# Two transformer blocks in one kernel: three token-major products in 512-column blocks, and sliding attention's value parts side by side

## The chip, the cores and the metric

The kernel runs on one core of a Trainium2 chip. The metric is device time in microseconds (us), the median of several executions. The engines are TensorE (PE, matrix products and transposes; its weight loads are shown as PEld), VectorE (DVE), ScalarE (ACT), GpSimd (POOL) and SyncE (SP, which issues most DMAs). PE writes its results to PSUM, which has eight banks of 512 float32 columns.

## The reference, cut to what matters

Two blocks run one after the other on 512 tokens of width 1024, batch 1, all in float32. The change touches the first block's mixer and its attention to a memory of 256 rows:

```python
def hybrid_mixer(x, w_in, ...):
    proj = x @ w_in
    ml_qk, ml_v, ml_o, ml_i, ml_f, sw_q, sw_k, sw_v = jnp.split(proj, IN_SPLITS, axis=-1)
    ml_qk = jax.nn.silu(causal_dwconv(ml_qk, ml_conv_w, ml_conv_b))
    ml_q, ml_k = jnp.split(ml_qk, 2, axis=-1)
    h_ml = mlstm(ml_q, ml_k, ml_v, ml_o, ...)        # 4 heads of 128; sigmoid(ml_o) gates the result
    h_sw = sliding_window_attention(sw_q, sw_k, sw_v, swa_sinks, rel_bias)   # 8 heads of 64, 2 value heads
    return jnp.concatenate([h_ml, h_sw], axis=-1) @ w_out

def memory_cross_attention(x, mem, wq, wkv, wo):
    q = (x @ wq).reshape(B, S, XA_HEADS, XA_HEAD_DIM)
    k, v = jnp.split(mem @ wkv, 2, axis=-1)
    ...
```

In the sliding attention a block of 128 tokens sees itself and the block before it, so block 0 has one block of keys and blocks 1 to 3 have two. The values and gate (`ml_v`, `ml_o`) are 512 columns each, memory's values are 1024.

## The kernel before

A large product is made of split operands. `split` (L111) makes a high part by an ACT copy that rounds, and a low part by a DVE subtraction; `mm3` (L137) then sums three passes in PSUM: high x high, high x low, low x high. Weights come from HBM in pieces of 1 MB into one of three `raw` buffers, issued by SP (`load_cols`, L101). `split_w` (L115) splits them into tiles `wh` and `wl` of 1024 columns, for each of which there are five buffers (`WB`, L91).

Values, gate and memory's values are token-major: the activations are the stationary operand, the weights the moving one. `tm_block` (L611) takes 256 columns: one load, two splits of four row blocks each, and `tm_cols` (L189), which computes two token tiles of 128 side by side in one bank, over all eight row blocks for one and then for the other. The values take two such blocks (`v_evac`, L595, an ACT copy into `vml`), the gate two (`o_evac`, L602, a tanh on ACT and a DVE operation into `og`), memory's values four (a split into `xvh`, `xvl`).

The sliding attention has eight groups, four token blocks by two value heads (`sw_group`, L520). A group makes scores of four heads in two banks with tag "s" (tile `sws`), a biased and negated copy with its minimum on DVE (L536, tile `swl`, three buffers), exponentials with sums on ACT (L541), a sum and a reciprocal on DVE (L543, L544), a scaling on POOL (L546), transposes on PE into a bank with tag "pt" (L551, tile `swpt`), their split (`swpth`, `swptl`), and the product with the values by `mm3` into the bank with tag "o" (tile `swop`). Of `swop`, DVE copies the upper and ACT the lower 64 partitions to `swo` (L562). The values `swv` were split at the start by `kv_evac` (L416), each head's 64 columns written twice, for the two halves of the partitions.

While the first mixer runs, the banks are: "mm" 0, 1, 2; "s" 3, 4; "pt" 5, 6; "o" 7 (`psm`, L342). `Banks` hands the banks of a tag out in turn, in the order in which the program names the tiles. The program's order is: projections of the sliding attention, its eight groups, values, gate, the query and key projections of the mixer's heads 0 and 1 (`cm_phase`, tile `cm`), memory's transposes, then for each head `ml_head` (L649; scores `mls`, numerators `num` in two "pt" banks, transposed result `htr` in the next "pt" bank) with memory's keys (`mem_key`, tile `mk`) between, then memory's values, then the mixer's output projection (`tm_rotate`, tile `tm`, all eight banks).

The order on each engine is not the program's: the compiler's scheduler plans it ahead with a timeline of its own, and takes of the instructions that are ready the one that stands first in the program. On the chip each engine then runs its list in order.

Of the kernel before, what the change touches and what calls it, by code (L numbers as in the profile page):

```python
# [8 lines left out]
F32 = mybir.dt.float32  # L9
F32R = mybir.dt.float32r  # L10
AF = mybir.ActivationFunctionType
OP = mybir.AluOpType
# [3 lines left out]
P = 128  # L16
T = 512
NT = T // P
D = 1024
KC = D // P  # L20
# [21 lines left out]
def tile_two_blocks(ctx: ExitStack, tc: tile.TileContext, a: dict, out: bass.AP, dbg=None):  # L42
    nc = tc.nc
    pe, act, dve, pool, sp = nc.tensor, nc.scalar, nc.vector, nc.gpsimd, nc.sync
# [48 lines left out]
    def raw_tile(name):  # L93
        return rawp.tile([P, 2112], F32, name=name, tag="raw", bufs=RAWB)
# [16 lines left out]
    def split(hi, lo, src):  # L111
        act.activation(hi, src, AF.Copy)  # L112
        dve.tensor_sub(lo, src, hi.bitcast(F32))  # L113

    def split_w(src, pl=None):  # L115
        shape = list(src.shape)
        n = 1
        for s in shape[1:]:
            n *= s
        if pl is None:  # L120
            hi = w_tile("wh")[:, :n]
            lo = w_tile("wl")[:, :n]
        else:
            pl, i = pl
            hi = pl.tile([P, n], F32R, name=f"wxh{i}")
            lo = pl.tile([P, n], F32R, name=f"wxl{i}")
        if len(shape) == 3:
            hi = hi.rearrange("p (k c) -> p k c", k=shape[1])
            lo = lo.rearrange("p (k c) -> p k c", k=shape[1])
        split(hi, lo, src)  # L130
        return hi, lo
# [5 lines left out]
    def mm3(ps, wh, wl, xh, xl, first, last):  # L137
        pe.matmul(ps, wh, xh, start=first, stop=False)  # L138
        pe.matmul(ps, wh, xl, start=False, stop=False)  # L139
        pe.matmul(ps, wl, xh, start=False, stop=last)  # L140
# [198 lines left out]
    w_in = a["w_in"][0]  # L339
    A0 = act_set(apool0, "x")  # L340
    psm = Banks(mm=(0, 1, 2), s=(3, 4), pt=(5, 6), o=(7,))
# [4 lines left out]
    mlq = open_pool("mlq", side="right")  # L346
    sw = open_pool("sw", side="left")
# [27 lines left out]
    swo = ml.tile([P, 4, T], F32, name="swo")  # L375
# [17 lines left out]
    while d0 < P:  # L393
        b = t5_bucket(d0)
# [10 lines left out]
    normg = sw.tile([P, T], F32, name="normg")  # L405
# [2 lines left out]


    swkt = [[sw.tile([P, P + T], F32R, name=f"swk{j}{i}") for i in range(2)] for j in range(2)]  # L410
    swv = [[sw.tile([P, 2, P], F32R, name=f"swv{t}{i}") for i in range(2)] for t in range(NT)]
    swk = [sw.tile([P, 2, 2, P], F32, name="swk", tag="swptl", bufs=2) for _ in range(2)]
    swk = [swk[t // 2][:, t % 2] for t in range(NT)]
    gates = [sw.tile([P, 8], F32, name=f"gates{t}") for t in range(NT)]

    def kv_evac(t, ps):  # L416
        kin = ps[:, 0:128].rearrange("p (j o d) -> p j o d", j=2, o=1).to_broadcast([P, 2, 2, 64])
        vin = ps[:, 128:256].rearrange("p (j o d) -> p j o d", j=2, o=1).to_broadcast([P, 2, 2, 64])
        dve.tensor_copy(gates[t], ps[:, 256:264])
        dve.tensor_copy(swk[t].rearrange("p j (u d) -> p j u d", u=2), kin)  # L420
        split(*[v.rearrange("p j (u d) -> p j u d", u=2) for v in swv[t]], vin)

    pst = Banks(tr=(3, 4, 5, 6), v=(7,))
    to_cm(pst, "tr", 4, xr[0][:, 0, :], A0, 0)
# [1 line left out]
    for k0, k1 in ((0, 3), (3, 6), (6, 8)):  # L426
        wh, wl = [w_tile(n)[:, :(k1 - k0) * 264].rearrange("p (k c) -> p k c", k=k1 - k0) for n in ("wh", "wl")]
        for j in range(0, k1 - k0, 2):
            e = min(j + 2, k1 - k0)
# [19 lines left out]
    for j in range(2):  # L449
        ps = psm.tile([P, T], F32, name="ktr", tag="pt", bufs=2)  # L450
# [6 lines left out]
    for g in range(2):  # L457
        ps = psm.tile([P, T], F32, name="gtr", tag="pt", bufs=2)
# [34 lines left out]
    ps = psm.tile([P, 14, 4], F32, name="actr", tag="pt", bufs=2)  # L493
# [26 lines left out]
    def sw_group(n, j):  # L520
        kbs = [0, 1] if n else [1]
        lo = 0 if n else P
        pts = {}
        Ps = []
        for cc in range(2):
            c = 2 * j + cc
            s = psm.tile([P, 2, 256], F32, name="sws", tag="s", bufs=2)
            for e in range(2):
                q = swq[2 * c + e][:, n * P:(n + 1) * P]
                for i in range(2):  # L530
                    pe.matmul(s[:, e, :], q, swkt[j][i][:, n * P:(n + 2) * P], start=i == 0, stop=i == 1)
            L = sw.tile([P, 2, 256], F32, name="swl", tag="swl", bufs=3)
            st = sw.tile([P, 5, 2], F32, name="swst", tag="swst", bufs=4)
            for e in range(2):
                h = 2 * c + e
                dve.tensor_tensor_reduce(L[:, e, lo:], s[:, e, lo:], swb[:, h, lo:], scale=-0.125,  # L536
                                         scalar=nsink[:, h:h + 1], op0=OP.add, op1=OP.min, accum_out=st[:, 1, e:e + 1])
            dve.tensor_sub(st[:, 2, :], st[:, 1, :], nsink[:, 2 * c:2 * c + 2])
            act.activation(st[:, 2, :], st[:, 2, :], AF.Exp)
            for e in range(2):  # L540
                act.activation(L[:, e, lo:], L[:, e, lo:], AF.Exp, scale=-1.0, bias=st[:, 1, e:e + 1],  # L541
                               accum_out=st[:, 3, e:e + 1])
            dve.tensor_add(st[:, 4, :], st[:, 3, :], st[:, 2, :])  # L543
            dve.reciprocal(st[:, 4, :], st[:, 4, :])  # L544
            for e in range(2):
                pool.tensor_scalar(L[:, e, lo:], L[:, e, lo:], st[:, 4, e:e + 1], 0.0, op0=OP.mult, op1=OP.add)  # L546
            Ps.append(L)
        for kb in kbs:
            pt = psm.tile([P, 4, P], F32, name="swpt", tag="pt", bufs=2)
            for h in range(4):  # L550
                pe.transpose(pt[:, h, :], Ps[h // 2][:, h % 2, kb * P:(kb + 1) * P], ident)  # L551
            pts[kb] = (sw.tile([P, 4, P], F32R, name="swpth", tag="swpth", bufs=2),
                       sw.tile([P, 4, P], F32R, name="swptl", tag="swptl", bufs=2))
            split(*pts[kb], pt)
        o = psm.tile([P, 2, 2, P], F32, name="swop", tag="o", bufs=1)
        for i, kb in enumerate(kbs):
            v, pt = swv[n - 1 + kb], [p.rearrange("p a b -> p (a b)") for p in pts[kb]]
            mm3(o.rearrange("p a b c -> p (a b c)"), v[0][:, j, :], v[1][:, j, :], pt[0], pt[1], i == 0,
                i == len(kbs) - 1)
        for e in range(2):  # L560
            r = slice(64 * e, 64 * e + 64)
            (act.copy if e else dve.tensor_copy)(swo[r, 2 * j:2 * j + 2, n * P:(n + 1) * P], o[r, :, e, :])  # L562

    NV = 31 + 3 + 3 + 4 + 4
    pv = consts.tile([P, 2, NV], F32, name="pv")
# [25 lines left out]
    og = ml.tile([P, 2080], F32, name="og", tag="og")[:, :NT * T].rearrange("p (t c) -> p t c", t=NT)  # L591
    vml = ml.tile([P, 2080], F32, name="vml", tag="vml").rearrange("p (t h c) -> p t h c", t=NT, h=4)
    pool.memset(vml[:, :, :, 128:130], 1.0)

    def v_evac(b):  # L595
        def f(t0, ps):
            for u in range(2):
                act.activation(vml[:, t0 + u, 2 * b:2 * b + 2, 0:128],
                               ps[:, u * 256:(u + 1) * 256].rearrange("p (h d) -> p h d", h=2), AF.Copy)
        return f  # L600

    def o_evac(b):  # L602
        def f(t0, ps):
            th = mlq.tile([P, 2, 256], F32, name="oth", tag="cy", bufs=2)
            act.activation(th, ps.rearrange("p (u c) -> p u c", u=2), AF.Tanh, scale=0.5)
            for u in range(2):
                dve.scalar_tensor_tensor(og[:, t0 + u, b * 256:(b + 1) * 256], th[:, u, :], 1.0,
                                         normg[:, b * 256:(b + 1) * 256], op0=OP.add, op1=OP.mult)
        return f

    def tm_block(w, c0, A, tt_n, psp, tag, bufs, evac):  # L611
        v = load_cols(w, c0, 256)
        ws = [split_w(v[:, k:k + 4, :]) for k in (0, 4)]
        tm_cols([(ws[k // 4][0][:, k % 4, :], ws[k // 4][1][:, k % 4, :]) for k in range(KC)], A, range(tt_n), 256,
                psp, tag, bufs, 2, evac)
# [18 lines left out]
            qk[c] = q  # L634
        return f

    for b in range(2):
        tm_block(w_in, 1024 + b * 256, A0, NT, psm, "mm", 3, v_evac(b))
    for b in range(2):
        tm_block(w_in, 1536 + b * 256, A0, NT, psm, "mm", 3, o_evac(b))  # L640
    dump("vml", vml)
    dump("og", og)

# [65 lines left out]
    M1 = act_set(apool1, "mem")  # L709
# [5 lines left out]
    wkv = a["xa_wkv"][0]  # L715
# [10 lines left out]
    for h in range(4):  # L726
        ps = ml_head(h)
# [19 lines left out]
    mlq.release()  # L747
    xvp = open_pool("xv")
    xvh, xvl = [xvp.tile([P, 2, D], F32R, name=f"xv{i}") for i in range(2)]
    for b in range(4):  # L750
        tm_block(wkv, D + b * 256, M1, 2, psm, "mm", 3,
                 lambda t0, ps, b=b: split(xvh[:, :, b * 256:(b + 1) * 256], xvl[:, :, b * 256:(b + 1) * 256],
                                           ps.rearrange("p (u c) -> p u c", u=2)))
    dump("h1h", H1[0].bitcast(F32))
    ml.release()

# [648 lines left out]
```

## Time and profile before

| | |
|---|---|
| time, median of 3 runs | 1320.43 us (1320.33 to 1323.15) |
| the profiled execution | 1322.3 us, of which its span 1320.6 |
| mean granted clock of PE | 0.994 |
| PE busy | 1300.4 us, 98% of the span, 6918 passes |
| DVE, ACT, POOL busy | 744.3, 534.2 and 76.1 us |

The views are read thus. A line of a timeline has the start in us from the span's start, the duration, the engine, the line of the kernel, the operation, the written and the read tiles by name, their shapes and a count. A PE pass is shown with a duration longer than its distance to the next one, since passes overlap. A line of a grouped view has busy time and mean duration of one (in ns) behind the first bar, and the engine's idle time before them behind the second.

### The profile page before, as it was taken

The page shows a single profiled execution, that of the slowest core. Times are in us where ns is not written, and L with a number is a line of the kernel's source. Part 1 is how long each engine was busy: PE and PEld are TensorE (multiplying, and loading weights), DVE is VectorE, ACT ScalarE, POOL GpSimd, SP SyncE. Part 2 cuts the span into 40 slices and gives each one's busy share as a digit, 9 for nine tenths or more (in the row PEclk, how much of TensorE's full clock was granted, in tenths as well). Part 3 has the DMA queues.
Part 4 walks back from the last instruction along what each step waited for, and adds up shares of the span by engine and source line. Part 5 has one row for each costly group of instructions (what it writes and reads, how often), then busy time and mean ns, then how long its engine had stood idle before and what let it go on. Part 6 is the DMA issues. An engine that isn't in the chain of part 4 may idle for free.

```text
span 1320.6 us, 17065 instructions
## 1 busy us (share of the span) xinstructions
PE 1300.4 (98%) x6918; PEld 1114.9 (84%) x6918; DVE 744.3 (56%) x1204; ACT 534.2 (40%) x895; POOL 76.1 (6%) x152
## 2 busy tenths in 40 slices
PE   8999999999999999999999999999999999999997
PEld 7899899899889888888888898767898888888886
DVE  5765877584666655556633569995453334532422
ACT  5664564333423433344422134576432223432311
POOL 3221020110000000000000120000100000000000
PEclk9999999998999999999999999999999999999999
DMA  8312344432223332313233124212234332223211
GB/s 255 108 65 73 104 144 160 181 109 97 97 96 116 124 128 64 128 64 128 70 122 128 32 69 138 73 45 93 73 93 125 96 96 97 96 96 112 96 46 51
DMA packets 92148, 134.87 MB, mean 102 GB/s; under 512 B 4572, under 2 KB 77329, under 8 KB 92062
## 3 DMA queue, kind: packets, MB, share of 16 engines
q1 hardware_dynamic: 90030, 129.09, 29.7%
q10 hardware_dynamic: 1384, 2.58, 0.6%
q0 software_dynamic: 656, 2.12, 0.5%
q8 instruction: 54, 0.88, 0.3%
q14 instruction: 24, 0.20, 0.0%
HBM read 131.66 MB, written 2.12 MB: 101 GB/s over the span
## 4 chain that ended last, share of the span: by engine, by line
PE 94%; DVE 3%; ACT 2%; issue 0%; DMA 0%; POOL 0%; SPq 0%; DVEq 0%; POOLq 0%; ACTq 0%
PE cm L139 15%; PE cm L138 15%; PE cm L140 15%; PE tm L224 9%; PE tm L223 9%; PE tm L227 9%; PE tmc L200 2%; PE tmc L201 2%; PE tmc L199 2%; PE tr L294 1%; PE tm L140 1%; PE tm L139 1%; PE tm L138 1%; PE num L680 1%; DVE cacc L1123 1%; PE mls L660 1%
## 5 line engine op out<-in xcount | busy, mean ns | idle before, releaser
L113 DVE TENSOR_TENSOR wl<-rawc,wh 128x1024 fp32r<-128x1024 f32 x140 | 170.7, 1222 | 203.6 <-ACT wh L112 203.3
L112 ACT ACTIVATE wh<-rawc 128x1024 fp32r<-128x1024 f32 x140 | 147.7, 1059 | 222.0 <-PE cm L139 190.8
L113 DVE TENSOR_TENSOR wl<-rawr,wh 128x1024 fp32r<-128x1024 f32 x73 | 88.9, 1223 | 147.4 <-ACT wh L112 147.4
L112 ACT ACTIVATE wh<-rawr 128x1024 fp32r<-128x1024 f32 x73 | 76.9, 1060 | 175.3 <-PE tm L227 126.6
L139 PE MATMUL cm<-x2l,wh 128*128 128x512 f32 (+1 forms) x392 | 143.8, 368 | 0.0
L140 PE MATMUL cm<-x2h,wl 128*128 128x512 f32 (+1 forms) x392 | 143.7, 367 | 0.0
L138 PE MATMUL cm<-x2h,wh 128*128 128x512 f32 (+1 forms) x392 | 143.1, 368 | 0.0
L139 PE MATMUL cm<-x4l,wh 128*128 128x512 f32 (+1 forms) x296 | 106.6, 361 | 1.3 <-DVE x4l L113 1.3
L140 PE MATMUL cm<-x4h,wl 128*128 128x512 f32 (+1 forms) x296 | 106.4, 360 | 0.0
L138 PE MATMUL cm<-x4h,wh 128*128 128x512 f32 (+1 forms) x296 | 105.9, 361 | 0.0
L140 PEld LDWEIGHTS cm<-x2h,wl 128*128 128x128 f32 x392 | 73.8, 189 | 12.1
L139 PEld LDWEIGHTS cm<-x2l,wh 128*128 128x128 f32 x392 | 73.8, 189 | 12.0
L138 PEld LDWEIGHTS cm<-x2h,wh 128*128 128x128 f32 x392 | 73.5, 189 | 12.3
L624 DVE SCALAR_TENSOR_TENSOR uy<-cm,fw,uy 128x511 f32<-128x511 f32 x88 | 65.5, 747 | 1.4
L138 PE MATMUL cm<-x3h,wh 128*128 128x512 f32 (+1 forms) x184 | 63.9, 352 | 1.1 <-DVE xc L624 0.8
L139 PEld LDWEIGHTS cm<-x4l,wh 128*128 128x128 f32 x296 | 55.8, 189 | 10.0 <-DVE x4l L113 1.5
L139 PE MATMUL cm<-x3l,wh 128*128 128x512 f32 (+1 forms) x184 | 64.1, 350 | 0.0
L140 PE MATMUL cm<-x3h,wl 128*128 128x512 f32 (+1 forms) x184 | 63.5, 347 | 0.0
L140 PEld LDWEIGHTS cm<-x4h,wl 128*128 128x128 f32 x296 | 55.8, 189 | 8.3
L138 PEld LDWEIGHTS cm<-x4h,wh 128*128 128x128 f32 x296 | 55.5, 189 | 8.5
L329 POOL TENSOR_TENSOR rs_r<-rs_e,mhalf 128x1 f32<-128x1 f32 (+1 forms) x16 | 24.2, 1510 | 540.5 <-DVE rs_e L328 540.5
L199 PE MATMUL tmc<-wh,xh 128*128 128x256 f32 (+1 forms) x160 | 47.2, 295 | 1.5 <-ACT wh L112 1.5
(457 smaller groups left out, 3058.2 us busy)
## 6 DMA issues: line engine op xcount, KB each, us to landing
rawc<-in_ffn_w_up_dram SPq DMA_DIRECT2D x22, 1024.0 KB
rawc<-in_w_in_dram SPq DMA_DIRECT2D x20, 1024.0 KB
rawc<-in_mlp_w_dram SPq DMA_DIRECT2D x16, 1024.0 KB
rawr<-in_mlp_w_dram SPq DMA_DIRECT2D x16, 1024.0 KB
rawr<-in_ffn_w_down_dram SPq DMA_DIRECT2D x11, 1024.0 KB
rawr<-in_w_out_dram SPq DMA_DIRECT2D x10, 1024.0 KB
rawc<-in_xa_wkv_dram SPq DMA_DIRECT2D x8, 1024.0 KB
rawc<-in_xa_wq_dram SPq DMA_DIRECT2D x4, 1024.0 KB
```

Of the source, the lines that this page charges most:

```text
L112: act.activation(hi, src, AF.Copy)
L113: dve.tensor_sub(lo, src, hi.bitcast(F32))
L138: pe.matmul(ps, wh, xh, start=first, stop=False)
L139: pe.matmul(ps, wh, xl, start=False, stop=False)
L140: pe.matmul(ps, wl, xh, start=False, stop=last)
L199: pe.matmul(o, xh, wh, start=k == 0, stop=False)
L200: pe.matmul(o, xh, wl, start=False, stop=False)
L201: pe.matmul(o, xl, wh, start=False, stop=k == KC - 1)
L223: pe.matmul(ps[t][h], xh, wh[:, c], start=i == 0, stop=False)
L224: pe.matmul(ps[t][h], xh, wl[:, c], start=False, stop=False)
L227: pe.matmul(ps[t][h], xl, wh[:, c], start=False, stop=i == n - 1)
L624: dve.scalar_tensor_tensor(dst[:, s:], ps[:, :T - s], w[:, j:j + 1], y[:, s:], op0=OP.mult, op1=OP.add)
```

## The change

Three things change.

- Values, gate and memory's values are computed by a new function, `tm_wide`, in blocks of 512 columns, one bank for each token tile. It loads half of the rows at a time (1 MB), splits two row blocks at once, and runs through all token tiles for each row block. The values use the banks "mm", "mm", "mm", "o", the gate "s", "s", "pt", "pt", memory's first column block "s", "s" and its second "pt", "pt".
- In the sliding attention the high and the low part of a value head stand side by side in 128 columns (one tile `swv` instead of two), so that one pass with the high and one with the low probabilities give the product of the high values in the upper and of the low values in the lower 64 partitions. Then ACT copies the lower half out, and two DVE additions add the halves into `swo`.
- The pool `sw` gets a small tile named "pad".

```diff
+    swv = [sw.tile([P, 2, P], F32R, name=f"swv{t}") for t in range(NT)]
...
+    sw.tile([P, 32], F32, name="pad")
...
+        vin = ps[:, 128:256].rearrange("p (j d) -> p j d", j=2)
...
+        v = swv[t].rearrange("p j (u d) -> p j u d", u=2)
+        split(v[:, :, 0, :], v[:, :, 1, :], vin)
...
         for i, kb in enumerate(kbs):
-            v, pt = swv[n - 1 + kb], [p.rearrange("p a b -> p (a b)") for p in pts[kb]]
-            mm3(o.rearrange("p a b c -> p (a b c)"), v[0][:, j, :], v[1][:, j, :], pt[0], pt[1], i == 0,
-                i == len(kbs) - 1)
+            for part in range(2):
+                pe.matmul(of, swv[n - 1 + kb][:, j, :], pts[kb][part].rearrange("p a b -> p (a b)"),
+                          start=i == 0 and part == 0, stop=i == len(kbs) - 1 and part == 1)
+        half_o = sw.tile([64, 2, 2, P], F32, name="swhalf", tag="swhalf", bufs=1)
+        act.copy(half_o, o[64:P])
         for e in range(2):
-            r = slice(64 * e, 64 * e + 64)
-            (act.copy if e else dve.tensor_copy)(swo[r, 2 * j:2 * j + 2, n * P:(n + 1) * P], o[r, :, e, :])
+            dve.tensor_add(swo[64 * e:64 * e + 64, 2 * j:2 * j + 2, n * P:(n + 1) * P], o[0:64, :, e, :],
+                           half_o[:, :, e, :])
...
+    def v_evac(t, ps):
+        act.activation(vml[:, t, :, 0:128], ps.rearrange("p (h d) -> p h d", h=4), AF.Copy)
+
+    def o_evac(t, ps):
+        th = mlq.tile([P, T], F32, name="oth", tag="cy", bufs=2)
+        act.activation(th, ps, AF.Tanh, scale=0.5)
+        dve.scalar_tensor_tensor(og[:, t, :], th, 1.0, normg, op0=OP.add, op1=OP.mult)
+
+    def tm_wide(w, c0, A, psp, banks, evac):
+
+        ps = [psp.tile([P, T], F32, name="tmw", tag=tag, bufs=bufs) for tag, bufs in banks]
+        for k0 in (0, 4):
+            v = raw_tile("rawv")[:, :4 * T].rearrange("p (k c) -> p k c", k=4)
+            sp.dma_start(v, w[k0 * P:(k0 + 4) * P, c0:c0 + T].rearrange("(k p) c -> p k c", p=P))
+            for k1 in (0, 2):
+                wh, wl = split_w(v[:, k1:k1 + 2, :])
+                for u in range(2):
+                    k = k0 + k1 + u
+                    for t, o in enumerate(ps):
+                        mm3(o, A[0][:, k, t * P:(t + 1) * P], A[1][:, k, t * P:(t + 1) * P], wh[:, u, :], wl[:, u, :],
+                            k == 0, k == KC - 1)
+        for t, o in enumerate(ps):
+            evac(t, o)
...
-    for b in range(2):
-        tm_block(w_in, 1024 + b * 256, A0, NT, psm, "mm", 3, v_evac(b))
-    for b in range(2):
-        tm_block(w_in, 1536 + b * 256, A0, NT, psm, "mm", 3, o_evac(b))
+    tm_wide(w_in, 1024, A0, psm, (("mm", 3), ("mm", 3), ("mm", 3), ("o", 1)), v_evac)
+    tm_wide(w_in, 1536, A0, psm, (("s", 2), ("s", 2), ("pt", 2), ("pt", 2)), o_evac)
...
-    for b in range(4):
-        tm_block(wkv, D + b * 256, M1, 2, psm, "mm", 3,
-                 lambda t0, ps, b=b: split(xvh[:, :, b * 256:(b + 1) * 256], xvl[:, :, b * 256:(b + 1) * 256],
-                                           ps.rearrange("p (u c) -> p u c", u=2)))
+    for b, tag in enumerate(("s", "pt")):
+        c = slice(b * T, (b + 1) * T)
+        tm_wide(wkv, D + b * T, M1, psm, ((tag, 2), (tag, 2)),
+                lambda t, ps, c=c: split(xvh[:, t, c], xvl[:, t, c], ps))
```

## Rows read from the trace of the kernel before

**Rows 1.** The page's chain of work that ended last: shares of the span by engine.

```profile
PE 94%; DVE 3%; ACT 2%; issue 0%; DMA 0%; POOL 0%; SPq 0%; DVEq 0%; POOLq 0%; ACTq 0%
```

**Rows 2.** Timeline of PE: start, duration, engine, line, out<-in, idle before.

```profile
118.77 0.28 PE L200 MATMUL tmc<-wl,xh 128*128 128x256 f32 x1
121.76 0.28 PE L201 MATMUL tmc<-wh,xl 128*128 128x256 f32 x1
...
170.05 0.40 PE L138 MATMUL cm<-xh,wh 128*128 128x512 f32 x1
173.93 0.39 PE L140 MATMUL cm<-xh,wl 128*128 128x512 f32 x1
```

**Rows 3.** PE by line, 50 to 122, then 205 to 233 us.

```profile
L199 PE MATMUL tmc<-wh,xh 128*128 128x256 f32 x128 | 37.1, 290 | 0.0
L531 PE MATMUL sws<-swk,swq 128*128 128x256 f32 x59 | 10.6, 289 | 1.3 <-DVE swq L515 1.3
L139 PE MATMUL swop<-swptl,swv 128*128 128x512 f32 x14 | 5.7, 404 | 0.0
...
L201 PE MATMUL tmc<-wh,meml 128*128 128x256 f32 x64 | 18.3, 285 | 0.0
```

**Rows 4.** Timeline, PE and ACT: first and last attention group's end, first projection.

```profile
66.49 0.39 PE L140 MATMUL swop<-swpth,swv 128*128 128x512 f32 x1
...
118.54 0.39 PE L140 MATMUL swop<-swpth,swv 128*128 128x512 f32 x1
...
119.42 0.37 ACT L562 COPY swo<-swop 64x256 f32<-64x256 f32 x1 [3.87 <-DVE swo L562]
...
121.88 0.40 PE L138 MATMUL cm<-xh,wh 128*128 128x512 f32 x1
```

**Rows 5.** Timeline of DVE, ACT and PE around the mixer's heads 0 and 1.

```profile
161.21 0.68 DVE L667 SCALAR_TENSOR_TENSOR pm<-mls,mle 128x512 f32<-128x512 f32 x1
165.18 0.60 DVE L694 SCALAR_TENSOR_TENSOR hn<-num,mv,og 128x128 f32<-128x128 f32 x2
...
177.85 0.58 ACT L737 ACTIVATE h0s<-htr 128x512 f32<-128x512 f32 x1
...
181.64 0.83 PE L680 MATMUL num<-vml,pm 128*128 128x130 f32 x6
```

**Rows 6.** All engines by line, 66.7 to 118.9 us: count, busy us, mean ns.

```profile
L546 POOL TENSOR_SCALAR swl<-swl,swst 128x256 f32<-128x256 f32 x22 | 11.0, 516 | 31.7 <-DVE swst L544 21.3 <-PE swpt L551 5.6 <-ACT swst L539 4.7
L541 ACT ACTIVATE swl<-swl,swst 128x256 f32<-128x256 f32 x20 | 10.0, 505 | 0.1
L113 DVE TENSOR_TENSOR swptl<-swpt,swpth 128x512 fp32r<-128x512 f32 x13 | 8.7, 685 | 3.0 <-ACT swpth L112 3.0
L536 DVE CUSTOM_DVE_ANT_0 swl<-sws,swb,nsink 128x256 f32<-128x256 f32 x20 | 8.7, 478 | 1.7 <-PE swpt L551 1.7
L112 ACT ACTIVATE swpth<-swpt 128x512 fp32r<-128x512 f32 x13 | 7.4, 595 | 4.2 <-PE swpt L551 4.1
L562 DVE COPY swo<-swop 64x256 f32<-64x256 f32 x7 | 2.9, 416 | 6.3 <-PE swop L140 6.3
L543 DVE TENSOR_TENSOR swst<-swst 128x2 f32<-128x2 f32 x10 | 1.4, 157 | 1.6 <-ACT swst L539 1.5
```

**Rows 7.** Timeline of PE, ACT, DVE: memory's first values, heads 2 and 3.

```profile
205.64 0.28 PE L199 MATMUL tmc<-wh,memh 128*128 128x256 f32 x1
208.27 1.05 PE L680 MATMUL num<-vml,pm 128*128 128x130 f32 x8
...
213.92 1.27 ACT L696 ACTIVATE hn<-hn,mf 128x128 f32<-128x128 f32 x4
...
229.09 0.60 DVE L694 SCALAR_TENSOR_TENSOR hn<-num,mv,og 128x128 f32<-128x128 f32 x2
```

**Rows 8.** Windows: length, busy (count) of PE, PEld, DVE, ACT, POOL; PE's clock; DMA.

```profile
850.00:860.00 10.00, 6.21 (x24) 3.03 (x22) 10.00 (x22) 5.77 (x11) 0.00 (x0) 1.00 0.54 204
860.00:870.00 10.00, 9.09 (x32) 6.84 (x33) 10.00 (x23) 5.04 (x10) 0.00 (x0) 0.83 0.01 2
```

More of the change, by code (lines that the diff above doesn't have):

```diff
@@ L410, in tile_two_blocks @@
     swkt = [[sw.tile([P, P + T], F32R, name=f"swk{j}{i}") for i in range(2)] for j in range(2)]
-    swv = [[sw.tile([P, 2, P], F32R, name=f"swv{t}{i}") for i in range(2)] for t in range(NT)]
+    swv = [sw.tile([P, 2, P], F32R, name=f"swv{t}") for t in range(NT)]
     swk = [sw.tile([P, 2, 2, P], F32, name="swk", tag="swptl", bufs=2) for _ in range(2)]
@@ L414, in tile_two_blocks @@
     gates = [sw.tile([P, 8], F32, name=f"gates{t}") for t in range(NT)]
+    sw.tile([P, 32], F32, name="pad")
     def kv_evac(t, ps):
         kin = ps[:, 0:128].rearrange("p (j o d) -> p j o d", j=2, o=1).to_broadcast([P, 2, 2, 64])
-        vin = ps[:, 128:256].rearrange("p (j o d) -> p j o d", j=2, o=1).to_broadcast([P, 2, 2, 64])
+        vin = ps[:, 128:256].rearrange("p (j d) -> p j d", j=2)
         dve.tensor_copy(gates[t], ps[:, 256:264])
         dve.tensor_copy(swk[t].rearrange("p j (u d) -> p j u d", u=2), kin)
-        split(*[v.rearrange("p j (u d) -> p j u d", u=2) for v in swv[t]], vin)
+        v = swv[t].rearrange("p j (u d) -> p j u d", u=2)
+        split(v[:, :, 0, :], v[:, :, 1, :], vin)
     pst = Banks(tr=(3, 4, 5, 6), v=(7,))
@@ L555, in sw_group @@
         o = psm.tile([P, 2, 2, P], F32, name="swop", tag="o", bufs=1)
+        of = o.rearrange("p a b c -> p (a b c)")
         for i, kb in enumerate(kbs):
-            v, pt = swv[n - 1 + kb], [p.rearrange("p a b -> p (a b)") for p in pts[kb]]
-            mm3(o.rearrange("p a b c -> p (a b c)"), v[0][:, j, :], v[1][:, j, :], pt[0], pt[1], i == 0,
-                i == len(kbs) - 1)
+            for part in range(2):
[3 more added lines that the diff above has]
+        act.copy(half_o, o[64:P])
         for e in range(2):
-            r = slice(64 * e, 64 * e + 64)
-            (act.copy if e else dve.tensor_copy)(swo[r, 2 * j:2 * j + 2, n * P:(n + 1) * P], o[r, :, e, :])
+            dve.tensor_add(swo[64 * e:64 * e + 64, 2 * j:2 * j + 2, n * P:(n + 1) * P], o[0:64, :, e, :],
+                           half_o[:, :, e, :])
     NV = 31 + 3 + 3 + 4 + 4
@@ L593, in tile_two_blocks @@
     pool.memset(vml[:, :, :, 128:130], 1.0)
[L595 to L609, printed above, removed]
+    def v_evac(t, ps):
[18 more added lines that the diff above has]
+            evac(t, o)
     def tm_block(w, c0, A, tt_n, psp, tag, bufs, evac):
```

## The prediction

> **What bounds the kernel now.** I read the page first, and in it the chain of work that ended last: TensorE (PE) carries 94% of it [rows 1]. So a microsecond of PE work taken out is a microsecond of time, as long as PE still finds other work in its place; and a microsecond for which PE runs dry is lost at once. Next I read the timeline of PE, for what one pass costs: from one start to the next, not by the duration shown, because the passes overlap. Last I read the two stretches that the change touches, 50 to 122 us and 205 to 233 us, by line, to see what lies between what.
>
> Start to start, 25 steps of a 256-column pass take 121.76 - 118.77 = 2.99 us, 0.1196 us each, and 17 steps of a 512-column pass take 173.93 - 170.05 = 3.88 us, 0.228 us each [rows 2]. A pass thus costs 0.108 us for 256 columns and about 0.012 us whatever its width.
>
> In the first stretch the 384 passes of values and gate (three lines of 128) stand between the score passes (59 of 64 lie in it), the 56 transposes and the value passes (three lines of 14) of the sliding attention [rows 3]. The first projection of queries follows the last of them at 121.88 [rows 4]. Until then PE never waits long: it takes a pass of values or gate whenever the attention, which stands earlier in the program, isn't ready. The attention's eight groups end their value passes from 66.9 (66.49 + 0.39) to 118.9 us (118.54 + 0.39) [rows 4]: seven steps of 7.4 us. PE's own work for a group of eight score passes, eight transposes and six value passes is only 8 x 0.12 + 0.96 (the transposes, put at what passes of 256 columns cost, more than they can) + 6 x 0.228 = 3.3 us. The attention is a long chain over four engines, and the 384 passes are its cover.
>
> **The change part by part.**
>
> Wide blocks: 384 passes become 192, 384 x 0.1196 - 192 x 0.228 = 2.1 us saved. Memory's values: 192 passes (three lines of 64 [rows 3]) become 96, 22.96 - 21.89 = 1.1 us saved. Value parts: 42 passes become 28, 14 x 0.228 = 3.2 us saved. Together 6.4 us of PE work.
>
> Here a rule of the Trainium skill speaks against the first two. It gives a warm pass as its columns over the clock plus about 2.5 ns (page "TensorE: Matmul & The Clock Gate", section "Wait — 56ns, not 53.3ns?"); by that, merging 288 pairs would save 0.7 us, an estimate from that page, where the rows give 2.1 + 1.1. The rows decide; the fixed part in this kernel is five times the page's.
>
> The order of the banks is where I part from the plain sum. The fourth value tile lies in bank 7 (tag "o"), which every attention group uses, and all eight groups stand ahead of it in the program. The gate's four tiles lie in the banks of the scores and of the transposed probabilities. Does a later tile get a bank that lies empty while an earlier one isn't ready? The mixer's heads answer. Head 1's second numerator uses the bank of head 0's first one. Head 0's last reading of its numerators ends at 165.78, and head 1's first operand was written at 161.89, yet its first six passes come at 181.64, after head 0's transposed result, which uses that bank in between, was copied out at 178.43 [rows 5]. The bank waited 16 us for its turn. I take it that banks go in program order.
>
> Then this follows. Three value tiles (banks 0 to 2) fill PE with 72 passes, 72 x 0.228 = 16.4 us. The fourth, 24 passes, waits for the last attention group to be copied out, and until its passes run none of the four split value weights is free. There are five buffers for these; the fifth takes the gate's first quarter, and the other three quarters, and all query projections behind them, wait. Gate passes on that first quarter (24) can run once score and transpose banks are free, in the attention's last group. So under the attention lie 16.4 + 5.5 us of cover in place of 46 us, and behind its end at F stand 24 value passes and 72 gate passes: 96 x 0.228 = 21.9 us. The query projections start at F + 21.9; now they start at 121.88. The break-even for this stretch is F = 100.0; now bank 7 is copied out at 119.79 [rows 4].
>
> How far does the attention shorten when PE is free for it? A chain sets a lower end: two score reductions on DVE, 0.96 us; two exponentials on ACT, 1.01; a sum and a reciprocal, 0.31; the scaling on POOL, 1.03 [rows 6]; eight transposes, 0.96: 4.3 us from one group's transposes to the next's, since with three buffers for the scores the next group's second half starts only then. DVE sets another: four reductions at 0.478, six small ones of about 0.157, two splits at 0.685, a copy at 0.416 [rows 6], 4.6 us. The change replaces DVE's copy and ACT's copy (0.37 [rows 4]) by an ACT copy of 64x512, bounded by 0.37 and the 0.6 of a 128x512 activation, and two DVE additions, each put like the copy, 0.416 [rows 6]; so DVE has 5.1 us a group. The upper end is 7.4, the step as it is. I take 5.1, DVE's sum: three PE steps of a chain no longer queue behind fillers, and most of the eight weight splits that lay between have moved behind it. The first step keeps 7.0, as cover is still there.
>
> F = 66.9 + 7.0 + 6 x 5.1 + 1.5 (0.6 + two additions and a handover) = 106.0. Projections start at 127.9 instead of 121.9: 6.0 us later, with the 2.1 and the 3.2 us already in it. The ends: with 4.3 in all steps F = 98.5 and the stretch ends 1.5 us earlier; with 7.4, F = 120.2 and it ends 20 us later.
>
> Memory's values: the first column block takes the score banks, free by then; the second the banks of the last head's numerators and transposes. From 205.64 [rows 7], 48 passes (10.9 us), heads 2 and 3 (14 numerator passes and a transpose, about 2 us) and the output projection's first 12 passes (2.7 us) last to about 221. If head 3's numerators come where they do now, their last reader ends at 229.69 [rows 7], and PE waits some 8 us. If they come as soon as head 2 allows (its passes end at 209.3, its result is scaled by 215.2 [rows 7], then 0.5 for four transposes, 1.3 for copy and split [rows 6], 1.8 for 14 passes (eight take 1.05 [rows 7]), 2 for the readers), the bank is free at about 221, and there is no wait. I take no wait, since their place now is behind filling passes and not behind data. So 1.1 us saved, at worst 7 lost.
>
> At nothing I put: the weight loads (eight of 1 MB each way, in longer pieces) and the splits (as many), both beside PE's work as now; the halved key and value copying at the start, at most 3 us of ACT and DVE beside PE's work; gate and value copying in fewer, longer instructions.
>
> Sum: +6.0 - 1.1 = 4.9 us. The profiled execution took 1322.3 us, 1320.6 of it the span; the median is 1320.43, 1.9 below. The difference is added to the median: 1325.3.
>
> **The rivals.**
>
> The full saving: PE finds cover after all (banks or weight buffers are given to whoever is ready, or the scheduler places the fourth tile otherwise), and the whole 6.4 us comes off: 1314.0. The point where it decides is the fourth tile: if its 24 passes and the later quarters of the gate run among the attention's, nothing is left behind F. For it: nearly all of the chain is PE's, and every removed pass is on it [rows 1]. Against it: the 16 us of [rows 5].
>
> The attention keeps up: steps of 4.6 us, DVE's sum without the additions. F = 66.9 + 7.0 + 27.6 + 1.5 = 103.0, the stretch loses 3.0, memory gives 1.1 back: 1322.3, no change that can be measured (about 0.2%, 2.6 us, is what a measurement of this kernel can tell). Should all steps reach 4.3 it would be 1317.8.
>
> Worse: the thinly used PE loses its clock. At 850 to 860 us PE was busy 6.2 of 10 us, and the next 10 us had a mean granted clock of 0.83, part of it at the lower level of 1.2 GHz [rows 8]. With the cover gone PE has 2.8 us of work (four value passes in place of six) in a step of 5.1, so it may happen here. At half the clock those 2.8 us double; three such steps cost 8 us: 1333. The Trainium skill describes the same for a kernel that waits between bursts (page "TensorE: Matmul & The Clock Gate", section "HAM oscillation — how this bites in real kernels"); the trace agrees by the row named.
>
> That the change doesn't do what it says is no rival: the counts follow from the diff.
>
> **How the numbers follow.** Forecast (PE runs dry, steps of 4.9 to 6): 0.50, of which 0.42 slower and 0.08 within 0.2%. Attention keeps up: 0.20, of which 0.14 within, 0.03 to each side. Full saving: 0.20, faster. Worse: 0.10, slower. So faster 0.23, within 0.2% 0.22, slower 0.55. The range takes in the full saving with a microsecond and a half below, 1312.5, and goes up to 1332, leaving out the worse case and the far bounds. The forecast's own range is 1322 to 1330, steps of 4.6 to 6.
>
> **What would show it.** In the profile of the changed kernel: value and gate passes of 512 columns, 192, and 96 of memory, 0.228 us apart; 28 value passes of the attention. Right, if the passes after about 75 us stand apart with idle time before score, transpose and value passes, if the fourth value tile's 24 passes come after the last attention group's copy, the gate's last 72 behind them, and the projections at about 128. Wrong, if passes of the fourth value tile or of the gate's later quarters stand among the attention's, or if the attention's last value pass comes before 98 us. For memory: idle PE between 219 and 230 us (shifted by the first stretch) would show the second stretch mis-sized.

## The result and the profile after

The changed kernel takes 1333.78 us (1333.55 to 1334.0) against 1321.79 us for the kernel before beside it: a ratio of 1.0088, with a 95% interval of 1.0074 to 1.0102. It is slower by 12 us, where 4.9 were forecast. The profiled execution has a span of 1332.0 us, 11.4 above that of the kernel before.

The chain of work that ended last, from the page of the changed kernel, where [rows 1] had PE at 94%:

```profile
PE 91%; DVE 4%; ACT 2%; DMA 1%; issue 1%; POOL 0%; SPq 0%; DVEq 0%; POOLq 0%; ACTq 0%
```

Next, windows of the same profile (stretch, length, busy time and count of PE, PEld, DVE, ACT and POOL, then PE's granted clock, DMA share and GB/s):

```profile
76.00:92.00 16.00, 12.22 (x63) 8.34 (x63) 14.15 (x61) 13.25 (x45) 6.08 (x13) 1.00 0.00 1
92.00:101.00 9.00, 6.71 (x32) 4.71 (x31) 5.35 (x20) 6.24 (x22) 2.60 (x8) 1.00 0.12 31
101.00:107.80 6.80, 6.17 (x17) 4.03 (x16) 2.12 (x4) 1.67 (x3) 0.82 (x2) 0.50 0.00 0
108.00:132.00 24.00, 23.41 (x103) 19.07 (x102) 10.80 (x12) 10.43 (x13) 0.00 (x0) 1.00 0.50 154
```

PE is busy 12.2 of 16 and then 6.7 of 9 us: the cover, value and gate passes that PE can take while the attention isn't ready, ran out at 76 us. From 101 to 107.8 us the granted clock is 0.50, the lower level of 1.2 GHz. From 108 us on PE is full again, with what had been left.

The timeline of PE shows the first attention group's last value pass, the last group's transposes and last value pass, and the first projection (columns as in [rows 2]). It answers to [rows 4], where these value passes came at 66.49 and 118.54 and the projection at 121.88:

```profile
67.50 0.40 PE L562 MATMUL swop<-swptl,swv 128*128 128x512 f32 x1
...
100.81 0.45 PE L553 MATMUL swpt<-ident,swl 128*128 128x128 f32 x2
...
104.78 0.63 PE L138 MATMUL tmw<-wh,xh 128*128 128x512 f32 x1
105.21 0.63 PE L139 MATMUL tmw<-wl,xh 128*128 128x512 f32 x1
...
107.34 0.61 PE L562 MATMUL swop<-swptl,swv 128*128 128x512 f32 x1
107.77 0.42 PE L138 MATMUL tmw<-wh,xh 128*128 128x512 f32 x1
...
131.78 0.39 PE L138 MATMUL cm<-xh,wh 128*128 128x512 f32 x1
```

The attention ends 11 us earlier than before, and yet the projections start 9.9 us later. At 105 us a pass takes 105.21 - 104.78 = 0.43 us in place of 0.228. The chain of waits tells what stood between (start, duration, what):

```profile
107.54 0.43 PE swop L562
...
108.33 0.59 ACT swhalf L565
108.94 0.42 DVE swo L567
109.37 0.43 DVE swo L567
109.94 0.47 PE tmw L138
```

The bank of the attention's last result is copied by ACT, read by two DVE additions, and free at 109.8; then come the value passes that waited for it. That is the fourth value tile.

The last value pass itself came late. Its second operand, the low part of the probabilities, was ready at 103.62 + 0.68 = 104.30, by the timeline of DVE:

```profile
103.62 0.68 DVE L113 TENSOR_TENSOR swptl<-swpt,swpth 128x512 fp32r<-128x512 f32 x1
```

But in PE's list six passes of the gate's first quarter stand ahead of it, from 104.78 to 107.34, each 0.43 us at the low clock: 2.6 us.

In the memory stretch, the timeline shows the first memory value pass, the first pass of the output projection (`tm`), the next memory value pass behind it, and the first query projection of the memory attention (`cm` on `x1h`; expectations below call it the second mixer's). Then come PE's waits at its weight loads between 216 and 240 us (us in total, times, longest):

```profile
216.11 0.39 PE L138 MATMUL tmw<-wh,memh 128*128 128x512 f32 x1
...
229.94 1.19 PE L138 MATMUL tm<-wh,h1h 128*128 128x512 f32 x4 [0.75 <-ACT wh L112]
...
238.64 0.39 PE L138 MATMUL tmw<-wh,memh 128*128 128x512 f32 x1
```

```profile
289.88 0.28 PE L138 MATMUL cm<-x1h,wh 128*128 128x256 f32 x1
```

```profile
PEld tm L139 <- DVE wl L113: 1.0, 1, 1.0
PEld tm L138 <- ACT wh L112: 0.9, 1, 0.9
PEld num L692 <- DVE bs L695: 0.6, 1, 0.6
```

From the first memory value pass to the query projection it takes 73.77 us. Before, it was 278.06 - 205.64 = 72.42 us, by this timeline and [rows 7]:

```profile
278.06 0.40 PE L138 MATMUL cm<-x1h,wh 128*128 128x256 f32 x2
```

So the span's 11.4 us are 9.9 in the first stretch, 1.35 in memory's, and a net 0.1 elsewhere.

### The profile page after: what moved, and what is told of

The parts are those of the page before. It is cut to its first block, busy times and chain, and to the rows that moved or that the text cites. A ratio compares the mean times of both kernels' runs of the same rounds, so it can differ in the third digit from the quotient of the medians.

```text
span 1332.0 us, 16478 instructions
## 1 busy us (share of the span) xinstructions
PE 1303.1 (98%) x6616; PEld 1097.8 (82%) x6616; DVE 748.0 (56%) x1208; ACT 536.7 (40%) x891; POOL 72.7 (5%) x152
## 4 chain that ended last, share of the span: by engine, by line
PE 91%; DVE 4%; ACT 2%; DMA 1%; issue 1%; POOL 0%; SPq 0%; DVEq 0%; POOLq 0%; ACTq 0%
PE cm L139 15%; PE cm L138 15%; PE cm L140 15%; PE tm L223 9%; PE tm L224 9%; PE tm L227 9%; PE tmw L138 1%; PE tmw L139 1%; PE tmw L140 1%; PE tr L294 1%; PE tm L139 1%; PE tm L140 1%; PE tm L138 1%; DVE wl L113 1%; PE tmc L200 1%
## 5 line engine op out<-in xcount | busy, mean ns | idle before, releaser
L113 DVE TENSOR_TENSOR wl<-rawc,wh 128x1024 fp32r<-128x1024 f32 x124 | 151.3, 1222 | 194.9 <-ACT wh L112 194.5
L112 ACT ACTIVATE wh<-rawc 128x1024 fp32r<-128x1024 f32 x124 | 131.0, 1060 | 218.8 <-PE cm L139 192.6
L138 PE MATMUL cm<-x4h,wh 128*128 128x512 f32 (+1 forms) x296 | 106.0, 361 | 0.6 <-DVE x4l L113 0.6
L1135 DVE SCALAR_TENSOR_TENSOR cacc<-zp,half,cacc 128x512 f32<-128x512 f32 x60 | 42.7, 744 | 0.2
```

The source lines that it names most:

```text
L1135: bg.append(lambda j=j: dve.scalar_tensor_tensor(acc[c], z[:, j:j + T], w[:, j:j + 1], acc[c], op0=OP.mult, op1=OP.add))
```

## Experiments

**One part at a time.** The first kernel has only the wide values and gate (the diff's `tm_wide`, its two calls in the mixer, and the two evacuations).

> The kernel before with only the first mixer's values and gate in 512-column blocks (fourth value tile in bank 7, gate in the score and transpose banks); sliding attention keeps its three value passes, memory its narrow blocks. Theory A (bank 7 and the held weight buffers put 96 passes behind the attention's end): value and gate passes run dry near 75 us, 90 or more of them stand behind the attention's end, the query projections start at 129 to 133 us (121.9 before, 131.8 with the whole change), time 1330 to 1333 against 1321.8. Theory C (the attention is slow in the changed kernel because of its new evacuation, a copy of half a bank and two additions): without it the attention ends at 103 or before, projections at 125, time 1325 or less. Theory B (what exceeded the forecast is the low clock of 101 to 108 us, and PE with six passes a group is busy enough to keep it): no low clock in the stretch, projections at 128, time 1328.

1329.24 us (1327.49 to 1333.1), ratio 1.0066 (1.0053 to 1.0079). Its timeline of PE, last group and first projection:

```profile
101.36 1.30 PE L551 MATMUL swpt<-ident,swl 128*128 128x128 f32 x6
...
104.82 0.39 PE L138 MATMUL tmw<-wh,xh 128*128 128x512 f32 x1
105.05 0.40 PE L139 MATMUL tmw<-wl,xh 128*128 128x512 f32 x1
...
106.45 0.40 PE L140 MATMUL swop<-swpth,swv 128*128 128x512 f32 x1
106.68 0.39 PE L138 MATMUL tmw<-wh,xh 128*128 128x512 f32 x1
...
129.82 0.39 PE L138 MATMUL cm<-xh,wh 128*128 128x512 f32 x1
```

The projections start 7.9 us later than before, at the full clock: a pass takes 0.23 us here. Theory C falls, since the attention ends at 106.9, not below 103, without the new evacuation. This part alone makes the kernel slower, and the projections lie where theory A puts them (129 to 133), the time 0.8 us below its range. The clock is full, as theory B wanted, and still the projections come 1.8 us later than it says. That clock is the one of the profiled execution; the last section has more on it.

The value parts alone (`swv`, `sw_group` and `kv_evac` of the diff):

> The kernel before with only the sliding attention's value parts side by side: two passes for three, and the copy of half a bank with two additions behind them. If PE's work sets the end of the stretch as long as its cover (the narrow values and gate) is there: 14 passes of 0.228 us less, projections 3.2 us earlier at 118.7, time 1318.6 against 1321.8. Theory C (the longer evacuation of bank 7 slows the attention): attention ends at 120 or later, projections at 122 or later, no gain or a loss, 1321.8 or more.

1319.67 us, ratio 0.9977 (0.9968 to 0.9987), 1.1 above the first expectation and below theory C's. Memory's values start 3.1 us earlier (202.50 against 205.64), as 14 passes of 0.228 us make it. Bank 7 comes free later than before (122.2 against 119.8 us), as theory C has it, and it doesn't matter, because PE has other work until then, as its timeline says:

```profile
118.62 0.40 PE L138 MATMUL cm<-xh,wh 128*128 128x512 f32 x1
...
119.08 0.39 PE L562 MATMUL swop<-swpth,swv 128*128 128x512 f32 x1
119.32 0.40 PE L139 MATMUL cm<-xl,wh 128*128 128x512 f32 x1
```

Projection passes (`cm`) lie on both sides of the last value passes. So this part is a gain where there is cover, and in the changed kernel it is none.

Memory's values alone (`tm_wide` and its two calls for memory):

> The kernel before with only memory's values in 512-column blocks, the first in the score banks, the second in the transpose banks. In the changed kernel the way from the first memory value pass to the second mixer's output lost 1.35 us where I forecast 1.1 us saved. Theory D (the transpose banks, which the heads' numerators and transposes use, hold the passes up): the same loss here, 1323 against 1321.8. Rival (the loss comes from the work before having been shifted by 10 us, so that loads and splits meet at other moments): the 1.1 us of saved PE work show, 1320.7.

1323.29 us, ratio 1.0012 (1.0004 to 1.0021). PE's waits at its weight loads, 205 to 240 us:

```profile
PEld tm L139 <- DVE wl L113: 1.0, 1, 1.0
PEld tm L138 <- ACT wh L112: 0.9, 1, 0.9
PEld num L696 <- DVE bs L699: 0.6, 1, 0.6
```

They are the three waits of the changed kernel to the tenth, with nothing shifted by 10 us: theory D's loss, not the rival's. The second column block's banks hold the last head's numerators; in the block's place the output projection's first passes (`tm`) are drawn forward, and wait there for their weights to be split. 2.5 us of waits against 1.1 us of passes saved make 1.4; by the timeline the way from memory's first value pass to the memory attention's query projections is 279.80 - 205.97 = 73.83 us, 1.41 above before.

**Bank 7 or the weight buffers.** In this kernel the fourth value tile is computed after the other three from the same weights, in one of the three "mm" banks:

```diff
-    tm_wide(w_in, 1024, A0, psm, (("mm", 3), ("mm", 3), ("mm", 3), ("o", 1)), v_evac)
+    mm = ("mm", 3)
+    tm_wide(w_in, 1024, A0, psm, (mm, mm, mm), v_evac, (mm,))
...
+        for t, (tag, bufs) in enumerate(late, len(ps)):
+            o = psp.tile([P, T], F32, name="tmw4", tag=tag, bufs=bufs)
+            for k in range(KC):
+                mm3(o, A[0][:, k, t * P:(t + 1) * P], A[1][:, k, t * P:(t + 1) * P], ws[k][0], ws[k][1],
+                    k == 0, k == KC - 1)
+            evac(t, o)
```

> The changed kernel with one thing other: the fourth value tile comes after the first three from the same weights, in bank 0, so that it waits neither for bank 7 nor for the end of the attention; the gate stays in the score and transpose banks, memory as changed. Theory A (the fourth value tile, in bank 7 and on held weight buffers, is what takes PE's cover away): the four value weight buffers come free near 82 us, PE takes projection passes between the attention's from then on, no 24 us of dry PE; PE work is 5.3 us below that of before, memory costs 1.4 to 1.8: 1318 to 1321. Rival (the gate's tiles in the attention's banks alone are enough to hold all behind the attention's end): 72 to 96 gate passes and then the projections behind it, 1329 to 1333.

In the next one the tile stays in bank 7, but needs no weight buffer:

```diff
+                        r = (A[0][:, k, :], A[1][:, k, :]) if banks[t][0] == "o" else (wh[:, u, :], wl[:, u, :])
```

> The changed kernel with the fourth value tile still in bank 7, but its 24 passes read the kernel's input as their second operand in place of the split value weights (so the values of the last 128 tokens are not computed; pass count, widths and banks are as changed). It no longer holds a weight buffer. Theory A1 (the held buffers carry the loss, because neither the gate's later quarters nor the query projections get a buffer): PE takes projection passes from about 76 us on, and little is left behind the attention's end; 1319 to 1323. Theory A2 (bank 7 itself carries it: its 24 passes and what stands behind them in the program come after the attention's end): as the changed kernel or up to 2 us better, 1331 to 1334.

They take 1327.9 us (ratio 1.0046, 1.0034 to 1.0058) and 1331.29 us (1.0069, 1.0057 to 1.0081), both far above what was expected of the theory that frees the buffers (1318 to 1321 and 1319 to 1323). The first is also 1.1 us below its rival's range. The second lies inside its rival's, A2's, and its interval overlaps that of the changed kernel, so its time doesn't speak for A1. Its trace does, for the cover. In both kernels the cover comes back: projection passes stand among the attention's from 84.9 and from 75.4 us on. Timeline of PE, the first kernel, then the second:

```profile
84.86 0.50 PE L138 MATMUL cm<-xh,wh 128*128 128x512 f32 x1
```

```profile
75.38 0.50 PE L138 MATMUL cm<-xh,wh 128*128 128x512 f32 x1 [0.27 <-ACT wh L112]
```

So the held buffers are what takes the cover away, as theory A1 says: freed of them, PE has cover even with the tile in bank 7. But the forecast gain didn't come. Windows of the first of the two:

```profile
130.00:140.00 10.00, 7.90 (x37) 6.33 (x36) 5.97 (x6) 6.07 (x8) 0.00 (x0) 1.00 0.16 41
140.00:150.00 10.00, 6.79 (x20) 5.24 (x21) 8.93 (x15) 4.14 (x7) 0.00 (x0) 0.66 0.52 170
```

What was won under the attention is given back behind it: 5.3 us without PE work, and a low clock after. The timeline of ACT there:

```profile
136.82 1.28 ACT L606 ACTIVATE oth<-tmw 128x512 f32<-128x512 f32 x2 [0.98 <-PE tmw L140]
...
138.94 1.44 ACT L643 ACTIVATE cy<-cm,mlw 128x512 f32<-128x512 f32 x2
140.27 0.60 ACT L112 ACTIVATE memh<-tr 128x512 fp32r<-128x512 f32 x1
```

The convolutions (`cy`) of projections whose passes ended near 102 us begin only at 138.94, behind the gate's last tanh (`oth`) and one weight split. Both use one ring of two buffers, and the gate stands first in the program. The split of memory's transposes (`memh`), for which PE waits 4.6 us, is queued behind them. The kernel without weights for the fourth tile has a stretch like it (PE busy 6.5 of 10 us from 140 to 150, at a clock of 0.66); it was not run with the ring changed, nor was the changed kernel with more weight buffers. To see whether the ring did it, one kernel takes the first of these two and gives the tanh the other ring:

```diff
-        th = mlq.tile([P, T], F32, name="oth", tag="cy", bufs=2)
+        th = mlq.tile([P, T], F32, name="oth", tag="cth", bufs=2)
```

> The kernel with only the fourth value tile in its own bank (1327.9), with one thing other: the gate's tanh goes into the ring of two buffers that the projections' tanh uses (cth), not into that of their convolutions (cy). In 1327.9 PE had cover through the attention, and then stood dry for 5.9 us at 137 to 144, when the convolutions of the early projections (done since 102) began only after the gate's last tanh. Theory E (the shared ring gave the gain back: a convolution, though its data is there, waits for the gate, and holds its bank and the engines' order behind it): the wait shrinks to 2 us or less, 1322 to 1325. Rival (the wait is the work of DVE and ACT itself, four gate pieces, two convolutions and a memory split, wherever the buffers lie): 1327 to 1329.

1322.97 us, ratio 1.0009 (0.9999 to 1.0019), inside theory E's range and 4.9 us below the kernel it changes. The windows of the stretch that was dry:

```profile
130.00:140.00 10.00, 10.00 (x45) 8.28 (x45) 4.46 (x5) 3.85 (x5) 0.00 (x0) 1.00 0.00 0
140.00:150.00 10.00, 10.00 (x45) 7.71 (x44) 8.46 (x13) 7.17 (x11) 0.00 (x0) 1.00 0.67 211
```

**The low clock.** To have PE busier in the attention's steps, each pair of score passes is done twice (`for i in (0, 1, 0, 1)` for `range(2)` in `sw_group`).

> The changed kernel with every pair of the sliding attention's score passes done twice (the second writes the same scores again): 64 passes of 0.12 us more, 7.7 us of PE work, nearly an extra microsecond in each of the attention's eight steps, so that PE is busier in them; all else as changed. Theory B (the low clock of 101 to 108 us makes most of the excess over the forecast): with PE busier no low clock in the stretch, the last group's passes are 3 to 3.5 us quicker, and only some of the added passes lie on the attention's chain (half a microsecond in each of the five dry steps at most): projections at 129 to 131.5, time 1331 to 1333.5, no later than the changed kernel although it does more. Rival (the low clock costs little, the steps are as long as they are by the chain over four engines): projections at 132 to 135, time 1334 to 1337.

1336.41 us, ratio 1.0111 (1.0098 to 1.0124); the projections come 1.8 us later than in the changed kernel (133.6). The low clock is gone, and the kernel is no faster: theory B's range is missed, the rival's is met. Timeline of PE, the last group:

```profile
104.32 0.38 PE L553 MATMUL swpt<-ident,swl 128*128 128x128 f32 x2
...
109.36 0.39 PE L562 MATMUL swop<-swptl,swv 128*128 128x512 f32 x1
109.58 0.39 PE L138 MATMUL tmw<-wh,xh 128*128 128x512 f32 x1
```

The rows do give the clock's price. From the last group's transposes to its last value pass's end it takes 107.77 - 100.81 = 6.96 us in the changed kernel. With the same passes at the full clock it takes 109.58 - 104.32 = 5.26 here, and with two value passes more 106.68 - 101.36 = 5.32 in the kernel of values and gate alone, 4.86 without those two. The low clock cost 1.7 to 2.1 us.

**Banks of their own, for all.** Values and gate both in banks 0 to 2, with the fourth tile last (the second call as the first above):

> The changed kernel, but values and gate both only in the three banks 0 to 2: three token tiles side by side, and the fourth after them from the same weights, in the next of the three banks. As many passes, loads and splits as the changed kernel. Theory A: PE has all 192 passes as cover again and none waits for the attention; the stretch loses its 24 us behind the attention's end, projections at 117 to 118 (5.3 us of PE work less than before), memory still 1.35 worse: 1317 to 1319. Rival (the attention itself, slowed by a PE that is always busy, sets the end: seven steps of 7.4 us end at about 120): projections at 122, time 1323. Rival (holding four of five weight buffers until the fourth tile is done is what hurts, whichever bank it has): PE runs dry between the values and the gate for some us, time 1325 or more.

1320.99 us, ratio 1.0003 (0.9994 to 1.0011), between theory A's 1317 to 1319 and the first rival's 1323. The 24 us behind the attention are gone, but memory's values start only 2.4 us earlier than before, not 5.3. PE's waits at its weight loads, 118 to 128 us:

```profile
PEld swop L562 <- ACT swpth L112: 1.6, 1, 1.6
PEld swpt L553 <- POOL swl L548: 1.5, 2, 1.3
```

Now the attention falls behind instead, further than the first rival's 120: PE is full up to 120 us, and bank 7 is free only at 137.5. Next, memory's values take banks 0 to 2 as well:

```diff
-    for b, tag in enumerate(("s", "pt")):
-        tm_wide(wkv, D + b * T, M1, psm, ((tag, 2), (tag, 2)),
+    for b in range(2):
+        tm_wide(wkv, D + b * T, M1, psm, (("mm", 3), ("mm", 3)),
```

> The kernel of own banks (values and gate in banks 0 to 2, the fourth tile after the other three) with memory's value blocks in banks 0 to 2 too, in place of the score and the transpose banks. Own banks took 1321.0; in its trace and in that of memory alone the way from the first memory value pass to the second mixer's projections is 1.7 to 1.8 us longer than before. Theory D (the second column block waits for the transpose banks, which the last head's numerators hold, and the output projection's first passes are pulled in front of it before their weights are split): in banks 0 to 2 nothing waits, the 1.1 us of saved PE work show in place of the loss, 1321.0 - 1.8 - 1.1 = 1318.1. Rival (wide blocks of half the token tiles lose by themselves, by their weight splits): 1321 as before.

1328.84 us, ratio 1.0049 (1.0037 to 1.0061): 8 us worse, outside both expectations. The passes of memory no longer wait, and stand earlier; the last head's last numerators come 10.75 us later in their place (232.77 against 222.02). Waits at PE's weight loads, 225 to 290 us:

```profile
PEld cm L139 <- DVE x1l L113: 2.2, 1, 2.2
PEld cm L138 <- DVE X L802: 1.7, 1, 1.7
PEld tm L138 <- ACT h1h L112: 1.3, 1, 1.3
```

The last head's result (split into `h1h`) and then the first normalised tile (`X`, `x1l`) are now what is late. So other banks alone don't give theory D's loss back. Last, own banks with memory's values narrow as before:

> The kernel of own banks (values and gate wide in banks 0 to 2, two value passes) with memory's values in narrow blocks as before. Theory D (wide memory blocks cost 1.7 us by the order they force on the last head and the output projection, whatever stands before them): 1321.0 - 1.7 = 1319.3, and the way from memory's first value pass to the second mixer's projections is 72.4 us again. Rival (the loss of memory alone, 1.3 us, is tied to what it meets there): 1320.5 to 1321.

1317.82 us, ratio 0.9967 (0.9955 to 0.998). By its timeline, memory's first value pass and the memory attention's first query projection:

```profile
202.58 0.28 PE L199 MATMUL tmc<-wh,memh 128*128 128x256 f32 x1
```

```profile
275.00 0.40 PE L138 MATMUL cm<-x1h,wh 128*128 128x256 f32 x2
```

72.42 us, to the hundredth what it was before. Theory D holds for the way; the time is 1.5 us below its 1319.3. The profile's span is 1316.3, 4.3 below that of the kernel before. With the gate narrow too:

> Value parts side by side, values in 512-column blocks in banks 0 to 2 with the fourth tile after them, gate and memory's values in narrow blocks as before. In the kernel of own banks the attention fell behind (bank 7 free at 137.5, 119.8 before) and PE waited 2.8 us for it at 121 to 126. Theory F (wide blocks stand before the attention's steps in runs of 20 to 26 passes, 4.6 to 6 us, and so slow it; the narrow gate's shorter pieces do less): the attention ends before 127, the 2.8 us wait is gone; PE work is 1.05 us above that of all wide (2.1 us for 192 pairs of passes, half of them), so 1321.0 - 1.7 (narrow memory) - 2.8 + 1.05 = 1317.6. Rival (the value part of the stretch is what delays the attention): a wait of some us remains, 1319.5 to 1322.

1318.68 us, ratio 0.9971 (0.9962 to 0.998). The attention's bank is free at 128.0, not before 127, and 1.3 us of waits remain of 3.1: theory F in direction, about half in size. These two and the value parts alone beat both kernels; among the three the intervals overlap.

## Why the prediction was right and wrong

**The mechanism: right.** PE ran dry under the attention, the fourth value tile came behind the attention's last copy (109.37 + 0.43, then `tmw` at 109.94), and the rest of the gate behind it. Of the gate's first quarter 18 passes ran under the attention and 6 behind it, where they hid bank 7's copy. The kernel of own banks shows that without this placing the loss of the first stretch is a gain of 2.4 us, and the trace of the one without weights in bank 7 shows that it is the held buffers that take the cover. By themselves two of the three parts lose: values and gate 7.9 us of the first stretch, where 6.0 were forecast with the value parts in it, and memory 1.4, where a gain of 1.1 was forecast.

**The tail behind F: right.** From F = 109.8 to the projections it took 131.78 - 109.8 = 22.0 us, 21.9 were forecast. A wide pass costs (131.78 - 109.94) / 96 = 0.228 us here too. The Trainium skill's fixed part of 2.5 ns a pass (page "TensorE: Matmul & The Clock Gate", section "Wait — 56ns, not 53.3ns?") is not what these rows show: 512 columns at 2.4 GHz are 0.213 us, the rest is 0.015.

**The attention's end: mis-sized.** The step that failed is "I take 5.1, DVE's sum" for the last six groups, with the clock left to a rival and the gate's 24 passes under the attention at no cost to it. F was forecast at 106.0 and is 109.8. The step from the first group's end to the second's took 6.8 us (7.0 forecast). The next six took 4.2, 5.4, 4.8, 5.6, 6.3 and 7.0, 33.2 in all, where six of 5.1 make 30.6; the start and the copying add 1.2. Of these 2.6 us of steps the low clock has 1.7 to 2.1. The six gate passes ahead of the last value pass take 2.6 of the last step; 1.2 of that is the low clock's share already counted, and 1.4 they would take at the full clock as well. So an operand that was ready waited behind cover in the list. The low clock is the rival "worse" in part: one stretch of it, not three steps, and on top of the forecast rather than in its place. That the rival's 1333 lies near the measured time is luck, for it has 8 us of clock in it. It was priced as a case by itself, with 0.10; it should have stood in the range of the dry case, because it is the dry case that leaves PE thinly used. DVE's sum of 5.1 us as the step is not confirmed: without the two additions, by values and gate alone, the six steps take 31.9 us, 5.3 each. What sets the other steps is not settled; DVE was busy 14.2 of 16 us between 76 and 92.

**Memory: wrong.** The step that failed is "I take no wait, since their place now is behind filling passes". I costed the head's numerators and not what is moved in front of the second column block: the output projection's first passes, with weights not yet split. -1.1 us were forecast, +1.35 measured; the price lay in the bounds (-1.1 to +7), the choice within them was wrong. Carried to the sum with the low clock beside it, these bounds would have taken the range's upper end of 1332 past the measured time.

**The sum.** 9.9 + 1.35 = 11.3 us against 6.0 - 1.1 = 4.9: 3.8 by the attention's end, 2.5 by memory, 0.1 by the tail. The rival of the full saving falls with its condition, since the later quarters of the gate did not run among the attention's passes.

**The value parts: right as a price.** 3.2 us were forecast, and alone they give 3.1 in the trace. In the stretch's 6.0 us they were no gain of their own, and rightly so. With PE dry there is nothing to save: the projections start at 131.78 with them and at 129.82 without, and the low clock, which only the profile with them has there, is about the difference.

## What to carry to other kernels

Before merging passes into wider ones, list what each wide block holds until its last pass (PSUM banks, and the split weights that its slowest tile still needs), and ask who behind it in the program gets none: 22 us of work were left behind the attention here, against 2 us saved in the passes. When cover returns, follow the ring buffers of what runs early: 4.9 us hung on one tag shared with a later stage. A move in one place is only priced once the instructions drawn forward into its place are priced too.

## What the runs showed of the hardware

The low clock is not read off from the busy share of a stretch. PE was busy 6.71 of 9 us before it fell in the changed kernel; the kernel of values and gate alone had 7.19 of 9 in the same stretch and kept the full clock, and the one with doubled scores had 7.25 of 10 from 100 to 110 us and kept it too (granted clock 1.00):

```profile
92.00:101.00 9.00, 7.19 (x33) 5.25 (x34) 5.40 (x21) 6.87 (x23) 3.06 (x7) 1.00 0.13 31
```

```profile
100.00:110.00 10.00, 7.25 (x30) 4.66 (x30) 4.57 (x10) 5.70 (x16) 1.23 (x3) 1.00 0.00 0
```

The Trainium skill says that a kernel which waits between bursts of passes loses its clock (page "TensorE: Matmul & The Clock Gate", section "HAM oscillation — how this bites in real kernels"); the changed kernel agrees with it (0.50 for 6.8 us), these two, which also wait between their passes, don't show it. PE's longest wait in these stretches is 1.46 us in the changed kernel and 0.66 and 1.19 in the other two; whether that decides is not shown. Executions of one kernel also differ in the clock: values and gate alone took 1327.49 us at a mean clock of 0.999 and 1333.1 at 0.992, so the full clock of its profile holds for that execution.
